# VectorE forms the delta-net output's low parts, layer 1 walks its keys by token tile, and the result leaves through transposes of the updated x

## The chip, the cores and the metric

The kernel runs on one core of one Trainium2 chip. The metric is the device time of one execution in microseconds (us); smaller is better. TensorE (PE) does the matmuls, VectorE (DVE), ScalarE (ACT) and GpSimd (POOL) the elementwise work, and SyncE (SP) issues the DMAs. A change of under about 0.2% (4 us) can't be told from no change in this kernel's measurements.

## The reference

Two layers (shared by a context pass of 128 tokens and a denoising step of 256 latent tokens, so 384 tokens in all, of width 1024). Per layer, cut to what matters:

```
mod = silu(cond) @ w_mod + b_mod                    # shift, scale, gate of both halves
h = rmsnorm(x) * (1 + sc1) + sh1
(dq, dk, dv, ..., aq, ak, av, mg) = split(h @ w_in)  # 13 parts
o_dn = rmsnorm(gated_delta_rule(...)) * silu(dgate)  # 8 heads of 128
y_a = o_dn @ w_br_dn                                 # delta net
y_b = (sb * conv3(scg * sx)) @ w_br_sc               # gated short convolution
y_c = attention(rope(norm(aq)), rope(norm(ak)), av) @ w_br_att
mix = (g_a*y_a + g_b*y_b + g_c*y_c) @ w_out
x = x + gt1 * rmsnorm(mix)
x = x + gt2 * rmsnorm(relu(h2 @ w_up)**2 @ w_down)   # h2: x normed and modulated again
```

The outputs are x after layer 1 (for both passes) and the context's keys, values and delta-net states.

## The kernel before, in words

**Tiles.** The 384 tokens are 3 token tiles of 128 (t = 0 context, t = 1, 2 latent). `xm` (tile name XT in the trace) holds x with tokens on partitions, 128 x 1024 for each token tile. `om` (tile name OT there) holds the output of a sub-layer in the same layout, and the name OT also serves `ot[f]`, the delta net's output of head f with channels on partitions, 128 x 384. PSUM tiles are `mm` (accumulators of the large products) and `ax` (small ones).

**Precision.** Each large product of fp32 operands is three fp32r matmuls: high x high, high x low, low x high. A high part is a cast (`ah`, `HH`, `wh`), a low part is the difference of the value and its high part (`al`, `HL`, `wl`). Weights come by DMA into `wr` (4 buffers); ACT casts `wh` and DVE subtracts `wl` (3 buffers each). `split(k, src)` does the same for an activation: ACT casts `ah`, POOL subtracts `al`. Small products are plain fp32 matmuls. One fp32 matmul is two MATMUL instructions in the trace, and one transpose is one instruction; the listing of an engine's instruction order, further down, counts each of either once.

**The modulation** of a layer is worked out while the layer before it (or the first half of the same layer) runs. Pieces of `w_mod` come through the same `wr` buffers. DVE sums them into `macc` (TENSOR_SCALAR and SCALAR_TENSOR_TENSOR, 128 x 1024), and 16 narrow matmuls `ax<-macc,one` add up the partitions; other pieces go to PE as they are, 16 at a time (8 in some places), as `ax<-wr,csil`. In the code both are the matmuls with a `tile_position`.

**Order.** All operations are recorded first, each with a class (`rec.cls`). `schedule()` then lists them engine by engine, with the durations that `cost()` gives and with the priority offsets of `PAR["off"]`; the resulting order of each engine is fixed, and only semaphores decide when an instruction starts. So a cost or a class that is changed moves instructions elsewhere too. `warmup()` gives one matmul on `ones` that the scheduler repeats in places where PE would idle at the end of the program; `cold(...)` names the last operation that they may precede.

**The keys of the attention** (`TM("k", l, 0, 272, evac_k)`): three weight pieces of `w_in` (816, 816 and 544 columns, so 3, 3 and 2 of the 8 blocks of 128 rows) times the three token tiles; 272 columns are 256 of keys and 16 of gates. The walk goes piece by piece: piece 0 for tiles 0, 1, 2, then piece 1, then piece 2, and with piece 2 each tile's sums are complete and `evac_k` norms and rotates the keys (`junk`, `kss`, `kn`, `ku`). The values follow in the same way (`evac_v`).

**The end.** After the last product of layer 1's MLP (`mm<-wh,u` and `mm<-wl,u`, 512 columns), each token tile goes through a chain: DVE multiplies the sums into `om`, ACT sums squares, DVE adds (m), POOL raises to the power -1/2, DVE refines by one Newton step (y, z in `ns`), and `finish_y` forms x + om * (z*y) and turns it, so that it is written with channels on partitions: 8 fp32 matmuls `xm` x ident start the sums (`ax<-ident,XT`), and 8 with the diagonal of z*y (`dg`) add om (`ax<-dg,OT`). ACT and DVE copy the two banks to `yst`, and a DMA writes them. A line of the profile's L1778 is the recorder's; every operation has it, so the tiles' names tell them apart.

Of the kernel before, what the change touches and what calls it, by code (L numbers as in the profile page):

```python
# [9 lines left out]
F32 = mybir.dt.float32  # L10
# [4 lines left out]
ADD, SUB, MUL = ALU.add, ALU.subtract, ALU.mult  # L15

P = 128
# [162 lines left out]
def cost(op, method, outs, ins, tag):  # L180

    n = max(size(v) for v in outs[:1] + ins)
    ps = any(tag.get(v.tensor.name) in PSUM_TAGS for v in outs + ins)
    if op.eng == "PE":
        n = size(outs[0])
        if tiled(op, ins):
            if "tile_position" in op.k:
                return n * 4 / 2.4 + 3 if op.k["tile_position"] == (0, 0) else 27.0
            return 43.0 if n <= 32 else 71.0
        if method == "transpose":  # L190
            return n * 2 / 2.4 + 3
        if ins[0].dtype == F32R and n >= 256:
            return n / 2.4 + 13.8
        return max(214.0, n * 4 / 2.4 + 3)
    if op.eng == "ACT":
        c = 51 + n * 0.833 + (0 if ps else 42)
        c += 93 * sum(isap(op.k.get(x)) for x in ("bias", "scale")) + 93 * (method == "mul")
        return c + (93 if "accum_out" in op.k else 0)
    if op.eng == "DVE":
        if method == "reciprocal":  # L200
            return 69 + 6.25 * n
        fast = method in ("tensor_scalar", "tensor_copy") and not ps
        sc = sum(isap(op.k.get(x)) for x in ("scalar", "scalar1", "scalar2"))
        return 69 + n * 1.042 * (0.5 if fast else 1) + 58 * sc
    if op.eng == "POOL":
        if method == "memset":
            return 35 + n * 0.833
        if method == "affine_select":
            return 160 + n * 0.83
        if method == "tensor_copy":  # L210
            return 250 if n <= 96 else 345
        return (165 + n * 2.1) if op.k.get("op") != ALU.pow else 300 + 165 * n
    return max(56.0, n * outs[0].shape[0] * 4 / 360.0)
# [24 lines left out]
def schedule(rec, par):  # L238
# [54 lines left out]
    while done < len(ops):  # L293
# [114 lines left out]
        **{(e, "w"): o for e, o in (("ACT", -500), ("DVE", 550), ("SP", 300))},  # L408
        **{(e, "bg"): o for e, o in (("PE", 950), ("DVE", 400), ("POOL", 800))},
        **{(e, "hv"): 1500 for e in ("PE", "ACT", "DVE")},  # L410
        ("DVE", "mv"): -200, ("DVE", "me"): 1000, ("PE", "gemm"): -1500,
    },
    "margin": 300.0, "gmargin": 0.0,
# [7 lines left out]
def build(tc, aps):  # L421
    nc = tc.nc
    rec = Recorder()
    PE, ACT, DVE, POOL, SP = (Eng(rec, n, r) for n, r in (
        ("PE", nc.tensor), ("ACT", nc.scalar), ("DVE", nc.vector), ("POOL", nc.gpsimd), ("SP", nc.sync)))
# [19 lines left out]
    def axtile():  # L445
        return pax.tile([P, 512], F32, tag="ax", name="ax")
# [41 lines left out]
    S = {}  # L488
# [89 lines left out]
                      start=True, stop=True)  # L578
        return rb

    def split(k, src):
        ACT.copy(a_hi[k], src)
        POOL.tensor_tensor(out=a_lo[k], in0=src, in1=a_hi[k].bitcast(F32), op=SUB)

    def warmup():

# [8 lines left out]
    def cold(first):  # L595
        if "fill" in S:
            S.pop("fill").last = rec.ops[first]
# [17 lines left out]
    def X(fn, *a):  # L615
        items.append(((), lambda _: fn(*a)))
# [26 lines left out]
    def G(keys, fn):  # L643
        items.append((tuple(keys), fn))
# [9 lines left out]
            rec.cls = "bg"  # L654
        G([("w", l, row)], run)

    def TM(kind, l, g, n, evac):

        st = {}

        parts = KPARTS if kind == "k" else HALVES

        def part(j):
            def run(ch):
                hi, lo = ch[0]
                if j == 0:
                    st["ps"] = [bank(), mmtile(), mmtile()]
                first = len(rec.ops)
                for t in range(3):
                    ps = st["ps"][t]  # L670
                    rec.cls = "gemm"
                    for i, k in enumerate(parts[j]):
                        ah = h_hi[k][:, t * P:(t + 1) * P]
                        al = h_lo[k][:, t * P:(t + 1) * P]
                        wh, wl = hi[:, i * n:(i + 1) * n], lo[:, i * n:(i + 1) * n]
                        PE.matmul(ps[:, :n], lhsT=ah, rhs=wh, start=k == 0, stop=False)
                        PE.matmul(ps[:, :n], lhsT=ah, rhs=wl, start=False, stop=False)
                        PE.matmul(ps[:, :n], lhsT=al, rhs=wh, start=False, stop=k == 7)
                    cold(first)
                    rec.cls = "bg"  # L680
                    if k == 7:
                        rec.cls = "ev"
                        evac(t, ps)
                        rec.cls = "bg"
            return run
        for j in range(len(parts)):
            G([(kind, l, g, j)], part(j))

    def TMW(keys, acts, evac, tail=False, after=None):

# [283 lines left out]
    def newton(n, c):  # L974

        rec.cls = "step" + S["u"]
        a, b, y, z, m = (n[:, c + j:c + j + 1] for j in range(5))
        DVE.tensor_tensor(out=m, in0=a, in1=b, op=ADD)
        POOL.tensor_tensor(out=y, in0=m, in1=mhalf, op=ALU.pow)
        DVE.scalar_tensor_tensor(out=z, in0=y, scalar=-0.5, in1=y, op0=MUL, op1=MUL)  # L980
        DVE.tensor_scalar(out=z, in0=z, scalar1=m, scalar2=1.5, op0=MUL, op1=ADD)
        return y, z

    def diag(t, y, z):
        dg = S["dg"][:, t]
        DVE.tensor_scalar(out=dg, in0=ident, scalar1=z, scalar2=y, op0=MUL, op1=MUL)
        rec.cls = "crit" + S["u"]
        return dg

    def finish_y(t, n):  # L990

        banks = [axtile() for _ in range(2)]
        cols = [(slice(f * P, (f + 1) * P), banks[f // 4][:, f % 4 * P:f % 4 * P + P]) for f in range(8)]
        for f, c in cols:
            PE.matmul(c, lhsT=xm[:, t, f], rhs=ident, start=f.start % 512 == 0, stop=False)
        dg = diag(t, *newton(n, 0))
        for f, c in cols:
            PE.matmul(c, lhsT=om[:, t, f], rhs=dg, start=False, stop=f.stop % 512 == 0)
            if t == 2 and f.start == 512:
                cold(len(rec.ops) - 1)  # L1000
        for g, ps in enumerate(banks):
            y4 = S["yst"][:, 4 * g:4 * g + 4, t * P:(t + 1) * P]
            p4 = ps.rearrange("p (f c) -> p f c", f=4)
            if g:
                DVE.tensor_copy(y4, p4)
            else:
                ACT.copy(y4, p4)
            SP.dma_start(aps["y"][:, 4 * g:4 * g + 4, t * P:(t + 1) * P], y4)
# [49 lines left out]
    def layer(l):  # L1058
# [518 lines left out]
        def evac_y(f, first):  # L1577
# [6 lines left out]
                    POOL.tensor_tensor(out=mix, in0=mix, in1=th, op=ADD)  # L1584
            return run

        def split_mix(f):
            DVE.tensor_scalar(out=xt[f], in0=xt[f], scalar1=0.5, scalar2=None, op0=MUL)
            split(f, xt[f])
# [27 lines left out]

        if l == 0:
            qkv(0)
        TM("k", l, 0, 272, evac_k)  # L1620
        TM("k", l, 1, 272, evac_v)
        X(gates)

# [43 lines left out]
                JOIN(("da", l, h))  # L1667
        spread = modlist(l, "M") if l == 0 else []
        for f in range(8):
            X(lambda f=f: split(f, ot[f]))  # L1670
        m2 = list(spread)

        due = [0.0]
# [200 lines left out]
```

## Time and profile before

| | |
|---|---|
| median of 3 runs | 1985.2 us (1985.07 to 1986.72) |
| the profiled execution | 1986.29 us, of which the span of the trace 1984.6 us |
| granted TensorE clock, mean | 0.997 |
| PE busy | 1957.0 us (99%) |
| DVE, ACT, POOL busy | 1405.9, 949.3, 431.6 us |
| moved by DMA | 280 MB, 141 GB/s on average |

Durations in a row are those of the instruction alone; PE pipelines its matmuls, so the time that one costs PE is the distance to the start of the next. In a timeline row "x8" groups 8 instructions that follow each other; the bracket at its end is the idle time of the engine before it, and what ended that.

### The profile page before, as it was taken

To read this page: it belongs to the slowest core of one execution; us is meant where nothing else is said; L and a number is where in the kernel's file an instruction comes from. 1 tells how busy PE (TensorE), PEld (TensorE's weight loads), DVE (VectorE), ACT (ScalarE), POOL (GpSimd) and SP (SyncE) were. 2 spreads that over 40 slices of the span, in tenths; PEclk is the share of its full clock that TensorE was granted. 3 is DMA by queue.
4 is the path that set the end of the run, shared out by engine and by line. 5 is a ranking of instruction groups with operands and counts; after the bars stand their busy time and mean duration, and the time that the engine had idled before them with its cause. 6 is when DMAs were issued, how large, how long until landed. Compare 5 with 4: busy or idle time off the path is not lost.

```text
span 1984.6 us, 35881 instructions
## 1 busy us (share of the span) xinstructions
PE 1957.0 (99%) x12980; PEld 1806.7 (91%) x12980; DVE 1405.9 (71%) x4317; ACT 949.3 (48%) x2188; POOL 431.6 (22%) x666
## 2 busy tenths in 40 slices
PE   9999999999999999999999999999999999999999
PEld 6998999999998799779779989999999998898987
DVE  3798887988868589769557988779888545432433
ACT  4676644555542354334246665445555424443432
POOL 1222222123234313003012022222232322110210
PEclk9999999999999999999999999999999999999999
DMA  8522333333336837756654223333333334554352
GB/s 270 192 81 84 106 110 130 119 122 117 107 124 208 289 128 231 217 189 204 158 177 147 85 94 115 111 119 122 121 115 107 120 123 144 195 124 128 127 128 64
DMA packets 132385, 280.48 MB, mean 141 GB/s; under 512 B 12240, under 2 KB 80496, under 8 KB 132208
## 3 DMA queue, kind: packets, MB, share of 16 engines
q1 hardware_dynamic: 132208, 278.19, 43.0%
q8 instruction: 102, 1.67, 0.3%
q14 instruction: 75, 0.61, 0.1%
HBM read 270.73 MB, written 7.42 MB: 140 GB/s over the span
## 4 chain that ended last, share of the span: by engine, by line
PE 83%; DVE 7%; DMA 4%; ACT 3%; issue 2%; POOL 0%; SPq 0%; DVEq 0%; ACTq 0%
PE mm L1778 70%; PE ax L1778 14%; DMA wr<-in_wmod 3%; DVE wl L1778 2%; DVE macc L1778 2%; ACT E L1778 1%; DVE q L1778 1%; ACT wh L1778 0%; DVE MB L1778 0%; ACT ht L1778 0%; ACT junk L1778 0%; DVE Xc L1778 0%; DVE Pr L1778 0%; DVE XT L1778 0%; DMA ws<-in_wmod 0%
## 5 line engine op out<-in xcount | busy, mean ns | idle before, releaser
L1778 DVE TENSOR_TENSOR wl<-wr,wh 128x1024 fp32r<-128x1024 f32 (+2 forms) x380 | 478.7, 1261 | 307.0 <-ACT wh L1778 305.8
L1778 ACT CAST wh<-wr 128x1024 fp32r<-128x1024 f32 (+2 forms) x380 | 396.0, 1043 | 559.3 <-PE mm L1778 454.1
L1778 PE MATMUL mm<-HH,wl 128*128 128x384 f32 x1664 | 568.9, 342 | 1.7 <-DVE wl L1778 1.7
L1778 PE MATMUL mm<-HL,wh 128*128 128x384 f32 x1664 | 567.7, 341 | 0.0
L1778 PE MATMUL mm<-HH,wh 128*128 128x384 f32 x1664 | 564.9, 340 | 0.6 <-ACT HH L1778 0.6
L1778 PEld LDWEIGHTS mm<-HH,wl 128*128 128x128 f32 x1664 | 312.9, 188 | 9.6 <-issue 4.5
L1778 PEld LDWEIGHTS mm<-HL,wh 128*128 128x128 f32 x1664 | 312.8, 188 | 6.5 <-issue 3.9
L1778 PEld LDWEIGHTS mm<-HH,wh 128*128 128x128 f32 x1664 | 312.4, 188 | 5.7 <-issue 1.2
L1778 DVE SCALAR_TENSOR_TENSOR macc<-wr,csil,macc 128x1024 f32<-128x1024 f32 x98 | 144.9, 1512 | 26.7 <-DMA wr<-in_wmod 26.7
L1778 PE MATMUL mm<-wh,HH 128*128 128x256 f32 (+1 forms) x480 | 139.9, 292 | 2.1 <-DVE eq L1778 1.4
L1778 PE MATMUL mm<-wl,HH 128*128 128x256 f32 (+1 forms) x480 | 139.4, 291 | 1.3 <-DVE wl L1778 1.3
L1778 PE MATMUL mm<-wh,HL 128*128 128x256 f32 (+1 forms) x480 | 140.1, 292 | 0.0
L1778 DVE TENSOR_TENSOR Pr<-MB,Xc 128x6 f32<-128x6 f32 (+30 forms) x496 | 138.7, 280 | 0.3
L1778 DVE TENSOR_REDUCE Xc<-Pr 128x6 f32<-128x12 f32 (+30 forms) x496 | 127.4, 257 | 7.7
L1778 DVE STREAM_SHUFFLE MB<-Mc 128x6 f32<-128x6 f32 (+30 forms) x496 | 131.7, 272 | 0.0
L1778 PE MATMUL mm<-al,wh 128*128 128x384 f32 x384 | 129.9, 339 | 1.6 <-POOL al L1778 1.5
L1778 PE MATMUL mm<-ah,wl 128*128 128x384 f32 x384 | 130.0, 339 | 0.2 <-DVE wl L1778 0.2
L1778 PE MATMUL mm<-ah,wh 128*128 128x384 f32 x384 | 130.0, 339 | 0.0
L1778 PE MATMUL mm<-wh,u 128*128 128x512 f32 x384 | 124.0, 399 | 0.0
L1778 PE MATMUL mm<-wh,ah 128*128 128x512 f32 x288 | 112.9, 392 | 0.0
L1778 PE MATMUL mm<-wh,al 128*128 128x512 f32 x288 | 112.7, 391 | 0.0
L1778 PE MATMUL mm<-wl,ah 128*128 128x512 f32 x288 | 112.5, 390 | 0.0
(270 smaller groups left out, 3314.8 us busy)
## 6 DMA issues: line engine op xcount, KB each, us to landing
wr<-in_wf SPq DMA_DIRECT2D x336, 512.0 KB, 3.3
wr<-in_wmod SPq DMA_DIRECT2D x80, 512.0 KB, 4.2
wr<-in_wq SPq DMA_DIRECT2D x16, 512.0 KB, 3.4
wr<-in_wdg SPq DMA_DIRECT2D x16, 512.0 KB, 3.3
ws<-in_wmod SPq DMA_DIRECT2D x16, 384.0 KB, 7.0
E<-scr SPq DMA_DIRECT2D x16, 384.0 KB, 3.6
Qe<-scr SPq DMA_DIRECT2D x16, 256.0 KB, 3.8
wr<-in_wkv SPq DMA_DIRECT2D x8, 408.0 KB, 5.7
```

What stands on the lines that cost most here:

```text
L1778: o.call(*o.a, **o.k)
```

## The change

Four edits.

1. `cost()`: a narrow matmul at `tile_position` (0, 0) is taken for 0.965 ns a column instead of 1.667. No instruction is added or removed by it; the scheduler's order changes.
2. The low parts of the delta net's output (8 for each layer, `al<-OT,ah`, 128 x 384) are subtracted by DVE instead of POOL, under a class "sp" of its own with an offset of 1000 on ACT and DVE.
3. In layer 1 the key product is walked by token tile: all 24 matmuls of tile 0 over the three weight pieces, then tile 1, then tile 2.
4. `finish_y`: DVE forms r = z*y and adds om * r into xm in two halves (SCALAR_TENSOR_TENSOR, 128 x 512), and 8 PE transposes turn the new xm; the 16 fp32 matmuls and the diagonal are gone.

```diff
@@ cost
-                return n * 4 / 2.4 + 3 if op.k["tile_position"] == (0, 0) else 27.0
+                return n * 0.965 + 3 if op.k["tile_position"] == (0, 0) else 27.0
@@ PAR["off"]
+        **{(e, "sp"): 1000 for e in ("ACT", "DVE")},
@@
-    def split(k, src):
+    def split(k, src, eng=POOL):
         ACT.copy(a_hi[k], src)
-        POOL.tensor_tensor(out=a_lo[k], in0=src, in1=a_hi[k].bitcast(F32), op=SUB)
+        eng.tensor_tensor(out=a_lo[k], in0=src, in1=a_hi[k].bitcast(F32), op=SUB)
@@ TM
-                hi, lo = ch[0]
...
-                    for i, k in enumerate(parts[j]):
...
+                    for (hi, lo), j in zip(ch, js):
+                        for i, k in enumerate(parts[j]):
...
-        for j in range(len(parts)):
-            G([(kind, l, g, j)], part(j))
+        n_ = len(parts)
+        for js in [tuple(range(n_))] if whole else [(j,) for j in range(n_)]:
+            G([(kind, l, g, j) for j in js], part(js))
@@ finish_y
-        banks = [axtile() for _ in range(2)]
-        cols = [(slice(f * P, (f + 1) * P), banks[f // 4][:, f % 4 * P:f % 4 * P + P]) for f in range(8)]
-        for f, c in cols:
-            PE.matmul(c, lhsT=xm[:, t, f], rhs=ident, start=f.start % 512 == 0, stop=False)
-        dg = diag(t, *newton(n, 0))
-        for f, c in cols:
-            PE.matmul(c, lhsT=om[:, t, f], rhs=dg, start=False, stop=f.stop % 512 == 0)
...
+        y, z = newton(n, 0)
+        r = n[:, 5:6]
+        DVE.tensor_tensor(out=r, in0=z, in1=y, op=MUL)
+        rec.cls = "crit" + S["u"]
+        for g in range(2):
+            ps = axtile()
+            h = slice(512 * g, 512 * g + 512)
+            DVE.scalar_tensor_tensor(out=xm[:, t, h], in0=om[:, t, h], scalar=r, in1=xm[:, t, h], op0=MUL, op1=ADD)
+            for j in range(4):
+                f = 4 * g + j
+                PE.transpose(ps[:, j * P:(j + 1) * P], xm[:, t, f * P:(f + 1) * P], ident)
...
@@ layer
+        def split_out(f):
+            rec.cls = "sp"
+            split(f, ot[f], DVE)
+            rec.cls = "bg"
...
-        TM("k", l, 0, 272, evac_k)
+        TM("k", l, 0, 272, evac_k, l > 0)
...
-            X(lambda f=f: split(f, ot[f]))
+            X(lambda f=f: split_out(f))
```

What the order of instructions becomes is shown at three places. First the end of PE's list, before; `mm<-wh,u` and `mm<-wl,u` are the last products of the MLP, `ax<-dg,OT` and `ax<-ident,XT` those of finish_y, `mm<-ones` the fillers:

```order
L1778 MATMUL ax<-dg,OT 128x128 x8
L1778 MATMUL ax<-ident,XT 128x128 x4
L1778 MATMUL ax<-dg,OT 128x128
L1778 MATMUL ax<-ident,XT 128x128 x4
L1778 MATMUL ax<-dg,OT 128x128 x7
L1778 MATMUL mm<-wl,u_3838 128x512
L1778 MATMUL mm<-wh,u_3838 128x512
L1778 MATMUL mm<-wh,u_3839 128x512
L1778 MATMUL mm<-wl,u_3839 128x512
L1778 MATMUL mm<-wh,u_3839 128x512
L1778 MATMUL mm<-ones 128x128 x17
L1778 MATMUL ax<-dg,OT 128x128 x8
```

The same end of PE's list, after:

```order
L1789 MATMUL mm<-wl,u_3838 128x512
L1789 MATMUL mm<-wh,u_3838 128x512
L1789 MATMUL mm<-wh,u_3839 128x512
L1789 MATMUL ax<-ident,XT 128x128 x4
L1789 MATMUL mm<-wl,u_3839 128x512
L1789 MATMUL ax<-ident,XT 128x128 x4
L1789 MATMUL mm<-wh,u_3839 128x512
L1789 MATMUL mm<-ones 128x128 x12
L1789 MATMUL ax<-ident,XT 128x128 x4
L1789 MATMUL mm<-ones 128x128 x5
L1789 MATMUL ax<-ident,XT 128x128 x4
L1789 MATMUL mm<-ones 128x128 x3
```

(A last `ax<-ident,XT` x8 follows.) Before, 24 fp32 matmuls stand ahead of the last five products; after, 8 transposes stand among them, and those of tile 1 stand among the fillers. The four groups of 4 `ax<-ident,XT` matmuls of tiles 0 and 1, which stood some 250 us ahead of the end in PE's list, have gone.

Second, DVE at the end of layer 0's delta net, before (`wl` and `macc` are the weights' low parts and the modulation's sums, `mgth` a gate):

```order
L1778 TENSOR_TENSOR wl<-wr,wh 128x1024
L1778 SCALAR_TENSOR_TENSOR mgth<-mgth,mm 128x384
L1778 SCALAR_TENSOR_TENSOR macc<-wr,csil,macc 128x1024 x4
L1778 TENSOR_TENSOR wl<-wr,wh 128x1024 x2
L1778 SCALAR_TENSOR_TENSOR macc<-wr,csil,macc 128x1024 x4
```

And after:

```order
L1789 TENSOR_TENSOR wl<-wr,wh 128x1024
L1789 TENSOR_TENSOR al_123<-OT,ah_115 128x384
L1789 TENSOR_TENSOR al_124<-OT,ah_116 128x384
L1789 TENSOR_TENSOR al_125<-OT,ah_117 128x384
L1789 TENSOR_TENSOR al_126<-OT,ah_118 128x384
L1789 TENSOR_TENSOR al_127<-OT,ah_119 128x384
L1789 TENSOR_TENSOR al_128<-OT,ah_120 128x384
L1789 TENSOR_TENSOR al_129<-OT,ah_121 128x384
L1789 SCALAR_TENSOR_TENSOR macc<-wr,csil,macc 128x1024
L1789 TENSOR_TENSOR al_130<-OT,ah_122 128x384
L1789 SCALAR_TENSOR_TENSOR macc<-wr,csil,macc 128x1024 x3
L1789 SCALAR_TENSOR_TENSOR mgth<-mgth,mm 128x384
```

The eight subtractions now stand ahead of the four sums and of the two `wl` that follow them.

Third, ACT at the start of layer 1's keys, before (`junk,kss` sums squares of the keys of one tile, `bt` its gates):

```order
L1778 COPY modrow<-ax 128x256
L1778 CAST wh<-wr 128x816
L1778 ACTIVATE junk,kss<-mm 128x128 x2
L1778 ACTIVATE bt<-mm 128x16
L1778 ACTIVATE junk,kss<-mm 128x128 x2
L1778 ACTIVATE bt<-mm 128x16
L1778 CAST wh<-wr 128x816
L1778 ACTIVATE bt<-mm 128x16
L1778 CAST wh<-wr 128x544
```

And after:

```order
L1789 ACTIVATE junk,kss<-mm 128x128 x2
L1789 ACTIVATE bt<-mm 128x16
L1789 ACTIVATE junk,kss<-mm 128x128 x2
L1789 ACTIVATE bt<-mm 128x16
L1789 ACTIVATE KTA<-ax,gqc 128x2x128
L1789 COPY modrow<-ax 128x256
L1789 CAST wh<-wr 128x816
L1789 ACTIVATE bt<-mm 128x16
L1789 ACTIVATE junk,kss<-mm 128x128
L1789 CAST wh<-wr 128x816
L1789 ACTIVATE junk,kss<-mm 128x128
L1789 CAST wh<-wr 128x544
```

The evacuations of tiles 0 and 1 now come ahead of the copy of `modrow`, and the three casts of the values' weights come behind it, one by one between those of tile 2.

## Rows read from the trace of the kernel before

**Rows 1.** The page: PE's busy time, and the chain that ended last by engine.

```profile
PE   1957.0 (99%) x12980; PEld 1806.7 (91%) x12980; DVE 1405.9 (71%) x4317; ACT 949.3 (48%) x2188; POOL 431.6 (22%) x666
...
PE 83%; DVE 7%; DMA 4%; ACT 3%; issue 2%; POOL 0%; SPq 0%; DVEq 0%; ACTq 0%
```

**Rows 2.** PE's waits by what ended them: us in total, times, longest.

```profile
PE ax L1778 <- DVE macc L1778: 7.9, 4, 4.2
...
PE mm L1778 <- POOL al L1778: 1.5, 2, 1.1
```

**Rows 3.** PE timeline, 33 us, then 1695 to 1708: start, us, instruction, [idle].

```profile
33.09 1.47 PE L1778 MATMUL ax<-ident,XT 128*128 128x128 f32 x12
...
1695.12 1.05 PE L1778 MATMUL ax<-ident,XT 128*128 128x128 f32 x8
...
1698.48 0.64 PE L1778 MATMUL ax<-wr,csil 128*32 128x256 f32 x8 [1.01 <-DMA wr<-in_wmod]
...
1706.66 1.05 PE L1778 MATMUL ax<-ident,XT 128*128 128x128 f32 x8
1707.55 0.38 PE L1778 MATMUL ax<-ident,modrow 128*128 128x128 f32 x2
```

**Rows 4.** PE timeline, the end of the program.

```profile
1968.13 1.95 PE L1778 MATMUL ax<-dg,OT 128*128 128x128 f32 x16
1969.91 1.10 PE L1778 MATMUL ax<-ident,XT 128*128 128x128 f32 x8
...
1973.45 0.48 PE L1778 MATMUL mm<-wl,u 128*128 128x512 f32 x1
...
1974.70 3.96 PE L1778 MATMUL mm<-ones 128*128 128x128 f32 x34
1978.49 1.99 PE L1778 MATMUL ax<-dg,OT 128*128 128x128 f32 x16
```

**Rows 5.** DVE timeline, the end of the program; then one group: busy, mean ns | idle.

```profile
1970.11 0.69 DVE L1778 COPY yst<-ax 128x512 f32<-128x512 f32 x1
...
1974.90 0.69 DVE L1778 TENSOR_TENSOR OT<-mm,OT 128x512 f32<-128x512 f32 x1 [0.48 <-PE mm L1778]
...
1977.58 0.16 DVE L1778 SCALAR_TENSOR_TENSOR ns<-ns 128x1 f32<-128x1 f32 x1 [0.44 <-POOL ns L1778]
...
1980.52 0.69 DVE L1778 COPY yst<-ax 128x512 f32<-128x512 f32 x1 [2.14 <-PE ax L1778]
...
L1778 DVE SCALAR_TENSOR_TENSOR XT<-OT,ns,XT 128x512 f32<-128x512 f32 x18 | 12.9, 748 | 0.3
```

**Rows 6.** Timelines of POOL, DVE and PE, 596 to 625; last a group of DVE.

```profile
598.38 9.78 POOL L1778 TENSOR_TENSOR al<-OT,ah 128x384 fp32r<-128x384 f32 x5
...
596.17 7.26 DVE L1778 SCALAR_TENSOR_TENSOR macc<-wr,csil,macc 128x1024 f32<-128x1024 f32 x4
...
620.30 4.87 DVE L1778 SCALAR_TENSOR_TENSOR macc<-wr,csil,macc 128x1024 f32<-128x1024 f32 x4 [0.94 <-DMA wr<-in_wmod]
...
604.33 0.44 PE L1778 MATMUL mm<-al,wh 128*128 128x384 f32 x1 [1.11 <-POOL al L1778]
...
605.41 0.45 PE L1778 MATMUL mm<-HH,wl 128*128 128x384 f32 x1 [0.29 <-DVE wl L1778]
...
608.22 0.45 PE L1778 MATMUL mm<-al,wh 128*128 128x384 f32 x1 [0.43 <-POOL al L1778]
...
L1778 DVE TENSOR_TENSOR al<-ax,ah 128x384 fp32r<-128x384 f32 x16 | 8.8, 552 | 5.4 <-ACT ah L1778 5.4
```

**Rows 7.** PE timeline, layer 1's keys, 1019 to 1050.

```profile
1028.69 0.64 PE L1778 MATMUL ax<-wr,csil 128*32 128x256 f32 x8 [0.95 <-DMA wr<-in_wmod]
...
1041.35 0.39 PE L1778 MATMUL mm<-wl,HH 128*128 128x272 f32 x1 [1.26 <-DVE wl L1778]
```

**Rows 8.** PE timeline; then a stretch: us, PE, PEld, DVE, ACT, POOL busy, PE clock, DMA.

```profile
853.30 1.06 PE L1778 MATMUL ax<-macc,one 128*32 128x256 f32 x2 [4.18 <-DVE macc L1778]
...
853.00:860.00 7.00, 6.70 (x26) 3.42 (x27) 2.58 (x3) 0.37 (x1) 0.00 (x0) 0.53 0.47 162
```

More of the change, by code (lines that the diff above doesn't have):

```diff
@@ L655, in FM, with TM, part @@
         G([("w", l, row)], run)
-    def TM(kind, l, g, n, evac):
+    def TM(kind, l, g, n, evac, whole=False):
         st = {}
         parts = KPARTS if kind == "k" else HALVES
-        def part(j):
+        def part(js):
             def run(ch):
-                hi, lo = ch[0]
-                if j == 0:
+                if js[0] == 0:
                     st["ps"] = [bank(), mmtile(), mmtile()]
@@ L671, in run @@
                     rec.cls = "gemm"
-                    for i, k in enumerate(parts[j]):
[L673 to L678, printed above, removed]
+                    for (hi, lo), j in zip(ch, js):
+                        for i, k in enumerate(parts[j]):
+                            ah = h_hi[k][:, t * P:(t + 1) * P]
+                            al = h_lo[k][:, t * P:(t + 1) * P]
+                            wh, wl = hi[:, i * n:(i + 1) * n], lo[:, i * n:(i + 1) * n]
+                            PE.matmul(ps[:, :n], lhsT=ah, rhs=wh, start=k == 0, stop=False)
+                            PE.matmul(ps[:, :n], lhsT=ah, rhs=wl, start=False, stop=False)
+                            PE.matmul(ps[:, :n], lhsT=al, rhs=wh, start=False, stop=k == 7)
                     cold(first)
@@ L990, in finish_y @@
     def finish_y(t, n):
-        banks = [axtile() for _ in range(2)]
-        cols = [(slice(f * P, (f + 1) * P), banks[f // 4][:, f % 4 * P:f % 4 * P + P]) for f in range(8)]
-        for f, c in cols:
-            PE.matmul(c, lhsT=xm[:, t, f], rhs=ident, start=f.start % 512 == 0, stop=False)
-        dg = diag(t, *newton(n, 0))
-        for f, c in cols:
-            PE.matmul(c, lhsT=om[:, t, f], rhs=dg, start=False, stop=f.stop % 512 == 0)
-            if t == 2 and f.start == 512:
-                cold(len(rec.ops) - 1)
-        for g, ps in enumerate(banks):
+        y, z = newton(n, 0)
[9 more added lines that the diff above has]
+                PE.transpose(ps[:, j * P:(j + 1) * P], xm[:, t, f * P:(f + 1) * P], ident)
+                if t == 2 and f == 4:
+                    cold(len(rec.ops) - 1)
             y4 = S["yst"][:, 4 * g:4 * g + 4, t * P:(t + 1) * P]
```

## The prediction

> **What bounds the kernel now.** I read the page first: PE is busy for 99% of the span, and the chain that ended last runs 83% through PE and 7% through DVE [rows 1]. Three readings follow. An instruction taken out of PE's list saves its distance to the next one's start, unless PE then waits for what follows. What DVE, ACT or POOL do is free, unless PE waits for it. And a shorter wait saves what it shortens. So I next read PE's waits: `macc` on DVE costs most, 7.9 us in 4 waits with the longest at 4.2; POOL's `al`, which edit 2 touches, costs 1.5 in 2 [rows 2]. Last I read the timelines of the stretches that the change touches, each engine beside the others: PE some 280 us before the end [rows 3], the end [rows 4, 5], layer 0's delta-net output [rows 6], layer 1's keys [rows 7].
>
> The sum is made against the profiled execution, 1986.29 us, of which the span is 1984.6 and 1.7 lies around it. It is 1.1 above the median of the runs, 1985.2, so 1.1 comes off at the end. About 0.2%, 4 us, is what a measurement can tell from no change.
>
> **Edit 4, away from the end.** The `ident` matmuls of tiles 0 and 1 are started early, in the middle of the MLP's products: 4 groups of 4 matmuls (x8 in the trace, two instructions each). One group starts at 1706.66, the next instruction at 1707.55: 0.89 us of PE [rows 3]. PE is the bound there, with matmuls on either side, so 4 x 0.89 = 3.6 us go. Behind the first of these groups stands a `ax<-wr,csil` that waits 1.01 us for its DMA at 1698.48 [rows 3]. PE would reach it 0.89 earlier and wait longer, were it not that edit 1 moves it behind some 6 to 9 more products. I estimate that 0.4 of that wait goes (0 to 1.0). Together -4.0.
>
> **Edit 4, at the end.** Before, PE spends 1968.13 to 1973.45, 5.3 us, on 24 fp32 matmuls (tile 0's and 1's with `dg`, tile 2's with `ident`) ahead of the last five products, which take 1973.45 to 1974.70 [rows 4]. Only those products complete tile 2's sums. After, 8 transposes stand among them. The nearest row for a transpose is the turning of x at the start, 12 in 1.47 us, 0.12 each or less [rows 3]: 8 cost at most 1.0. So the products are through at 1968.13 + 1.25 + 1.0 = 1970.4, 4.3 us earlier than 1974.70.
>
> What is late next is DVE, whose list I replay. It now does r and two halves x + om*r for each tile; such a half is in the trace in the other sub-layers, 748 ns [rows 5]. Tile 0's second half ends at about 1969.1, its transposes at 1970.1, and its copy to `yst` (0.69, as at 1970.11 [rows 5]) stands ahead of tile 2's first step, which so starts at 1970.85, against 1974.90 [rows 5]. Before, from there to the Newton step took 1977.58 - 1974.90 = 2.7 us [rows 5]; one of tile 1's halves now stands inside and adds up to 0.75 less what waits there anyway: Newton at 1973.9. Then 0.4 for it and r, two halves at 0.75, so tile 2's new x is ready at 1975.7.
>
> PE meanwhile has 20 fillers at 3.96/17 = 0.23 us [rows 4], 4.7 us, and 8 transposes of tile 1 at 0.12, 1.0: from 1970.4 it is free at 1976.0. The two paths end almost together. Then 8 transposes, to 1976.9, and the last copy starts near 1977.0 instead of 1980.52 [rows 5]: **-3.6**. The copy and the DMA behind it are the same. If the halves cost more or the replay slips by one instruction of 0.75, -2.8; if fillers are no obstacle, -4.2. The cover of the early transposes is thin: each 0.1 that PE or DVE loses here is lost at the end.
>
> **Edit 2.** In layer 0, POOL makes 8 low parts, the last 5 in 9.78 us, 1.96 each, while DVE's sums beside them take 7.26/4 = 1.82 each; where POOL is idle, at 620, they take 4.87/4 = 1.22 [rows 6]. PE waits for the last low parts and for a `wl` that DVE is late with: 1.11 + 0.29 + 0.43 = 1.8 us [rows 6]. After, DVE does them: the nearest DVE row is the same subtraction from PSUM, 552 ns [rows 6], so 8 cost 4.4 us. Queued behind them are four sums and two `wl`. But the sums get back 4 x 0.6 = 2.4 when POOL stands aside, and seven low parts fit into idle time that DVE has before the sums start. By that the low parts are there by 598, the sums end near 601.5 instead of 603.4, and `wl` behind them is ready before its use at 605.4. The three waits vanish: **-1.8**. Bounds: -2.3 (the small gaps around them go too), and, if the sums' chain is later by all of the 4.4 less 2.4, +2.0 wherever PE next waits for `macc`. At 620.30 DVE waits 0.94 for a DMA [rows 6], so a part of such a delay would be absorbed; I stay near the gain. In layer 1 PE shows no wait of this kind (both in rows 2's count are in layer 0), so edit 2 is worth nothing there.
>
> A rule speaks against this edit. The Trainium skill, "Perfetto Trace Analysis", section "Optimizing Scalar/DVE Operations", says that DVE and GpSimd share an SBUF read port, so that moving operations between those two might not help. By it edit 2 would be worth 0 instead of -1.8, and the result 1.8 later. The rows agree with the sharing (1.82 against 1.22), and just for that reason I expect a gain here: the same subtraction takes 1.96 on POOL and 0.55 on DVE, so moving it ends the sharing sooner.
>
> **Edit 3.** In layer 1, tile 0's keys are complete some 10 us earlier, since PE doesn't walk all three tiles first. The number of matmuls is the same. Before, PE waits 0.95 for a `ax<-wr,csil` and 1.26 for the values' first `wl` [rows 7]; the latter because ACT casts the values' weights only after it has copied `modrow`, and DVE subtracts after that. After, the casts stand behind the same copy and behind tile 0's and 1's evacuations, and the keys' `wh` buffers come free only in tile 2's walk. So the wait of 1.26 shrinks, as DVE has less else to do then, but it doesn't go. I estimate 0.6 of it left, and 0.3 of the wait of 0.95 gone with the later place: **-0.9**, between +0.6 (ACT's casts late by another 1.5) and -2.2 (both waits gone). POOL and DVE now rotate tile 0's keys earlier, and the delta net's first heads of layer 1 are reordered behind that; that is worth 0 on PE as long as PE has products to do, and I leave 1 us either way.
>
> **Edit 1.** No work changes. Some groups of narrow matmuls stand a few products later in PE's list, which helps where they wait for a DMA or for `macc` [rows 2] and hurts nothing that PE waits for. But DVE's orders change too (two `wl` in a row where one was). A product of 384 columns is 0.17 us, so a group that moves by three gains 0.5 where it waits, and there are the 4 for `macc` [rows 2] and a few like that of 0.95 [rows 7], of which one is long: at 853.30 PE waits 4.18 us for `macc`, and its clock then is at 0.53 for the 7 us from 853, the lower of its two levels for most of it (1.2 of 2.4 GHz), which costs another 7 x 0.47 = 3.3 [rows 8]. That wait comes from DVE waiting for a DMA, and moving the group by a few products shortens it by as much. I take **-0.5**, from -2 to +2 without that wait.
>
> The sum: 4.0 + 3.6 + 1.8 + 0.9 + 0.5 = 10.8. 1986.3 - 10.8 = 1975.5, less 1.1 is 1974.4; I say **1974.5 us**.
>
> **The rivals.**
> (A) The forecast, 1974.5, chance 0.54.
> (B) Only edit 4 counts; what edits 2, 3 and 1 gain is given back where PE next waits for `macc`, because its chain (DMA, sums, next DMA into the buffer that a sum has freed) is serial and doesn't hang on PE. For it: the largest wait is of that chain [rows 2]. Against it: DVE's sums get faster by edit 2. 1986.3 - 7.6 - 1.1 = 1977.6, chance 0.25.
> (C) The clock. In the last stretch transposes take the place of fp32 matmuls. If PE's clock fell on them, as it did behind the 4.18 us of waiting [rows 8], 24 transposes of 0.12 would take twice as long: up to 2.9 on the end, 1 at least for the last 8, which nothing covers. 1975.5 to 1977.4, chance 0.07. The Trainium skill, "TensorE: Matmul & The Clock Gate", section "Part 4: PE-mode transpose", says that a transpose doesn't count as PE being busy in the way a matmul does. Against it: the 12 transposes at 33 us show no more than 0.12 each [rows 3], and at the end fillers stand between.
> (D) The long wait goes. If the sums reach PE in time at 853, 4.2 + 3.3 = 7.5 go as well [rows 8]: 1967.0, chance 0.05. For it: edit 2 takes POOL off DVE's back. Against it: that is 250 us earlier.
> (E) The slower end: DVE's 4.4 us in layer 0 stand ahead of the sums, the buffers that these free are refilled later, and further groups `ax<-macc,one` wait as the one at 853 does, each with the wait and the clock behind it, 7.5 us [rows 8]. One such wait gives 1982.0, within 0.2%; two give 1989.5, slower. From a delay of the chain of 4 us or more it decides; my replay gives less than 0. Chances 0.05 and 0.03.
> (F) The change doesn't do what it says at the end: the transposes wait for DVE's halves ahead of the products that follow them in PE's list, so the last products are late by as much, and the end gains only 1 us instead of 3.6: 1977.1, chance 0.01 beyond what B holds.
>
> **How the numbers follow.** Range: the low end takes edits 1 to 3 at their good bounds (2.3, 2.2 and 2, so 3.3 more than in the sum) and the end at -4.2: near 1970.5, and I go to 1970.0. The high end takes B and the bad bounds of edits 2 and 4 (2.0 and 0.8): 1980.4, so 1980.5. D and E, 0.13, lie outside. Faster by over 0.2% (under 1981.2): A, B, C, D and F, 0.92, of which I move 0.03 to the same for noise in the sum: 0.89. Within 0.2%: one wait of E and that, 0.08. Slower: 0.03.
>
> **What the profile after would show.** Right: no `ident` groups near 1700, and PE's list shorter by 3.6 there; the last copy about 3.5 earlier relative to the last products of tile 1; no wait for `al` near 604 and sums of 1.2 us there; a wait of about half a us or less at the values' first `wl`; the wait at 850 still about 4. Wrong: further waits `PE ax <- DVE macc`; a clock below 0.9 in the last 10 us ahead of the last transpose; transposes of tile 0 that wait for XT; a new wait in layer 1's delta-net heads. The forecast is wrong above all if the order that edit 1 gives meets the DMAs differently at 853: one such wait more or less is as much as two thirds of the sum.

## The result, and the profile after

The changed kernel takes 1964.6 us (median of 4 runs, 1964.1 to 1966.2), against 1986.0 for the kernel before (4 runs); the ratio is 0.990, with an interval from 0.988 to 0.992. That is 21 us by the medians (20 by the ratio) where the prediction had 11, and below the range, whose low end was 1970.0. The profiled execution has a span of 1962.4 us against 1984.6, which is 22.2 less. A second series, on another occasion, gave 0.989 (0.987 to 0.991).

The page, PE's busy time and the chain that ended last by engine, of the changed kernel (as [rows 1]):

```profile
PE 1944.9 (99%) x12922; PEld 1797.9 (92%) x12922; DVE 1415.9 (72%) x4339; ACT 948.4 (48%) x2188; POOL 404.9 (21%) x650
...
PE 85%; DVE 7%; DMA 3%; ACT 3%; issue 1%; POOL 1%; SPq 0%; DVEq 0%; ACTq 0%; POOLq 0%
```

PE is the bound as before, busy for 12 us less and idle for 10 less. Its waits (as [rows 2]):

```profile
PE ax L1789 <- DVE macc L1789: 3.8, 4, 2.1
...
PE mm L1789 <- DVE wl L1789: 1.0, 2, 0.6
```

`macc` has gone from 7.9 to 3.8, and `al` is no longer in the list.

To see where the 22 us lie I took, from both traces, the start of the same large product (the n-th `mm` matmul, fillers not counted; there are 9024 in each) at some places, and compared how long the stretches between them last. All tables below are made so, in us against the profiled execution of before; the stretches are named by its times.

| stretch | what is there | change |
|---|---|---|
| 0 to 588 | start, layer 0's heads (edit 1 changes orders up to 50) | -2.3 |
| 588 to 656 | delta net's output split (edit 2) | -4.0 |
| 656 to 818 | layer 0's merge, MLP | +0.4 |
| 818 to 873 | layer 0's MLP: the long wait for `macc` | -6.1 |
| 873 to 1007 | layer 0's MLP | -0.7 |
| 1007 to 1320 | layer 1's keys, first heads (edits 3, 1) | -2.7 |
| 1320 to 1663 | layer 1 | +0.7 |
| 1663 to 1724 | early groups of finish_y, some 280 us ahead of the end (edit 4) | -4.6 |
| 1952 to the end | the end (edit 4) | -3.0 |

**The end.** PE's timeline there (as [rows 4]), and DVE's (as [rows 5]):

```profile
1949.62 0.60 PE L1789 MATMUL ax<-ident,XT 128*128 128x128 f32 x4
1949.97 0.48 PE L1789 MATMUL mm<-wl,u 128*128 128x512 f32 x1
...
1950.96 2.84 PE L1789 MATMUL mm<-ones 128*128 128x128 f32 x24
1953.64 0.60 PE L1789 MATMUL ax<-ident,XT 128*128 128x128 f32 x4
...
1955.62 0.83 PE L1789 MATMUL mm<-ones 128*128 128x128 f32 x6
1956.30 1.08 PE L1789 MATMUL ax<-ident,XT 128*128 128x128 f32 x8
```

```profile
1951.53 0.68 DVE L1789 TENSOR_TENSOR OT<-mm,OT 128x512 f32<-128x512 f32 x1
...
1955.19 1.42 DVE L1789 SCALAR_TENSOR_TENSOR XT<-OT,ns,XT 128x512 f32<-128x512 f32 x2
1956.52 0.68 DVE L1789 COPY yst<-ax 128x512 f32<-128x512 f32 x1
1957.42 0.69 DVE L1789 COPY yst<-ax 128x512 f32<-128x512 f32 x1 [0.21 <-PE ax L1789]
```

Four transposes take 1949.97 - 1949.62 = 0.35 us of PE, 0.09 each. With 19.2 us off by then, tile 2's first step at 1951.53 stands where 1970.7 would be before (1970.85 in the prediction), the last halves end at 1956.6 or 1975.8 (1975.7), the last copy starts at 1957.42 or 1976.6 (1977.0). The replay held to within 0.4 us. The span gains 0.9 less than the copy does: 4.3 us lie between the end of the last copy and the end of the span, before 3.4. In the trace of before the two last copies end 5.8 us or more behind those of tile 1; now the last three end within 1 us, and their DMAs of 256 KB follow each other. That the last DMA takes longer for this reason is argued, not tested.

**Where edit 2 is.** DVE and POOL in the stretch of [rows 6]:

```profile
591.27 3.36 DVE L1789 TENSOR_TENSOR al<-OT,ah 128x384 fp32r<-128x384 f32 x7
...
596.22 3.67 DVE L1789 SCALAR_TENSOR_TENSOR macc<-wr,csil,macc 128x1024 f32<-128x1024 f32 x3
```

The subtractions take 3.36/7 = 0.48 each, the sums 3.67/3 = 1.22, as where POOL was idle before, and PE doesn't wait there at all (590 to 620).

**The long wait.** The counterparts of [rows 8], PE's timeline and the same stretch of the program:

```profile
844.23 0.62 PE L1789 MATMUL ax<-macc,one 128*32 128x256 f32 x2 [0.99 <-DVE macc L1789]
...
853.00:860.00 7.00, 7.00 (x33) 5.82 (x33) 3.71 (x3) 3.14 (x5) 0.00 (x0) 1.00 0.45 157
```

0.99 us instead of 4.18, and a clock of 1.00 behind it instead of 0.53. The prediction held it for unlikely (D, 0.05) and had priced it at 7.5 us. It is one execution; further on, a second trace of the same kernel has the wait again.

### The profile page after: what moved, and what is told of

Its sections match the earlier page's. It is cut to its first block, busy times and chain, and to the rows that moved or that the text cites. A ratio compares the mean times of both kernels' runs of the same rounds, so it can differ in the third digit from the quotient of the medians.

```text
span 1962.4 us, 35757 instructions
## 1 busy us (share of the span) xinstructions
PE 1944.9 (99%) x12922; PEld 1797.9 (92%) x12922; DVE 1415.9 (72%) x4339; ACT 948.4 (48%) x2188; POOL 404.9 (21%) x650
## 4 chain that ended last, share of the span: by engine, by line
PE 85%; DVE 7%; DMA 3%; ACT 3%; issue 1%; POOL 1%; SPq 0%; DVEq 0%; ACTq 0%; POOLq 0%
PE mm L1789 72%; PE ax L1789 14%; DVE wl L1789 2%; DMA wr<-in_wmod 2%; DMA wr<-in_wf 1%; DVE macc L1789 1%; ACT wh L1789 1%; DVE MB L1789 1%; DVE Xc L1789 1%; DVE Pr L1789 1%; POOL xe L1789 0%; ACT E L1789 0%; ACT ht L1789 0%; DMA E<-scr 0%; DVE XT L1789 0%
```

## The experiments

Ratios are to the kernel before, run beside each kernel on the same chip, with their 95% intervals; 1% is 20 us. The kernel before had medians of 1987 to 1989 us there, between 1980 and 1998.

### Each edit alone

Only the lines of one edit of the diff are in each of these four.

**Edit 1** (`n * 0.965 + 3` in `cost()`):

> Edit 1 alone: only the cost of the narrow matmuls in the planner is changed, so the order of PE, DVE, SP and ACT differs, mostly in layer 0's MLP and from layer 1's keys on. Theory 1 (the 4.18 us wait for macc near 850 and the half clock behind it went because edit 1 puts wl and macc in another order on DVE there): the wait at 850 falls to about 1 us with the clock at 1.0, and the time is 6 to 8 us below before. Theory 2 (it went because edit 2 relieves DVE at 600 and the chain of sums arrives earlier): the wait stays near 4 us and the time is within 2 us of before. Theory 3 (the wait comes and goes from run to run, whatever the kernel): the two traces disagree with the timed runs.

Measured: 0.9955 (0.9942 to 0.9967), some 9 us. Other than the description of the change says, the edit does add instructions: the planner sets four more fillers (`mm<-ones`, 294 instructions in the trace instead of 286), in the first 26 us.

**Edit 2** (`split_out`):

> Edit 2 alone: the low parts of the delta net's output on DVE, all else as before. Both theories: no wait for al near 604, 3 to 4 us gained by 620. Theory 1: the wait near 850 stays about 4 us with the half clock behind it, time 2 to 4 us below before. Theory 2: the wait near 850 falls to about 1 us, time 8 to 10 us below before.

Measured: 0.9985 (0.9976 to 0.9994), some 3 us.

**Edit 3** (`TM(..., l > 0)`):

> Edit 3 alone: layer 1's keys walked by token tile. My sum had 0.9 us for it (from +0.6 to -2.2). The trace of the whole change shows about 1.9 less between 1010 and 1095, part of which may be edit 1's: expected 0.5 to 2 us below before. Theory 1 and theory 2 alike: the wait near 850 stays at about 4 us, since nothing ahead of 1010 is different.

Measured: 0.9978 (0.9965 to 0.9990), some 4 us.

**Edit 4** (`finish_y`):

> Edit 4 alone: the end through VectorE and transposes. My sum had 3.6 for the early groups and 3.6 at the end, 0.4 for a DMA wait: 7.2 to 7.6 us below before. If the DMA wait behind the first of the early groups grows by what the group took (0.9) as nothing shifts the group of narrow matmuls, 6.3 to 6.7. The wait near 850 stays at about 4 us.

Measured: 0.9969 (0.9957 to 0.9981), some 6 us.

The four ratios multiply to 0.989, which is what the whole change has: within the intervals (0.001 for each edit, 0.002 for the whole) the edits add up, and no gain is seen that only their combination brings. The largest is edit 1, for which the sum had 0.5 us. By stretches:

| stretch | edit 1 | edit 2 | edit 3 | edit 4 | whole |
|---|---|---|---|---|---|
| 588 to 656 | +0.6 | -4.1 | -0.2 | +0.7 | -4.0 |
| 656 to 818 | -0.3 | +1.2 | +1.4 | +2.8 | +0.4 |
| 818 to 873 | -5.6 | -2.2 | -4.6 | -3.8 | -6.1 |
| 1007 to 1320 | -2.0 | -0.1 | -3.1 | +0.2 | -2.7 |
| 1320 to 1663 | +0.9 | +0.1 | +0.7 | +0.1 | +0.7 |
| 1663 to 1724 | -1.0 | +0.3 | +1.1 | -4.2 | -4.6 |
| 1952 to the end | 0.0 | 0.0 | 0.0 | -3.0 | -3.0 |

Edits 2 and 4 have their places, to 0.5 us. But edits 3 and 4 change no order ahead of 1007, and yet gain 4 us at 818 to 873. So the profiled execution of before was a bad one there, and one trace of each kernel isn't enough to read that stretch. This is what the next runs are for.

### The same kernels again, and edit 1 in halves

A second trace of the kernel before:

> The kernel before once more, for a second trace. Its orders are those of before, so any difference of stages is what one execution differs from another. Theory 1 (the long wait near 850 belongs to the order of before): the wait for macc there is again 2.5 us or more, with or without the half clock. Theory 3 (it comes by chance whatever the order): it may be 1 to 1.6, as in the two traces that have edit 1.

The whole change without edit 1:

> The whole change without edit 1 (costs of the narrow matmuls as before). If the edits add up by their own runs (0.9955 x 0.9985 x 0.9978 x 0.9969 = 0.989 for all), this one has a ratio near 0.993, 13 to 14 us below before, and its wait for macc near 840 is 2.5 us or more. If edit 2 or 4 removes the wait too, the time is within 2 us of the whole change (ratio 0.99) and the wait is near 1.

Measured: 0.9927 (0.9910 to 0.9944), as the edits' own ratios gave. PE's wait that ends at 849.5 is 3.0 us. So edits 2 to 4 don't bring edit 1's gain.

Edit 1 for the matmuls on `macc` alone, and for those on the weight pieces alone:

```diff
-                return n * 4 / 2.4 + 3 if op.k["tile_position"] == (0, 0) else 27.0
+                c = 0.965 if any("macc" in v.tensor.name for v in ins) else 4 / 2.4
+                return n * c + 3 if op.k["tile_position"] == (0, 0) else 27.0
```

> Edit 1 for the matmuls on macc alone: the other narrow matmuls keep the cost of before. It changes the orders in layer 0's MLP (some 50 rows of PE, 40 of DVE) and little else. Theory 1: the wait near 850 falls to 1 to 1.6 us with the clock at 1.0, 3 to 6 us gained between 818 and 873, nothing elsewhere. If not the order there but the other narrow matmuls bring edit 1's gain: within 1 us of before outside of that stretch and no gain in it.

Measured: 0.9967 (0.9952 to 0.9982), some 6.5 us; the other half, with `not any(...)`:

> Edit 1 for the narrow matmuls on the weight pieces alone (those on macc keep the cost of before). It changes the orders from layer 1's keys on. Theory 1: the wait near 850 stays at 2.5 us or more; 0.5 to 1.5 us gained at the keys and 1 us near 1697, at most 2 to 3 us below before.

Measured: 0.9976 (0.9963 to 0.9990), some 5 us, more than expected; its trace shows only 2.4, of which 1.7 at 1007 to 1663.

Edit 1, the whole change and before once more, and the whole change without edit 3:

> Edit 1 alone once more, beside these on the same chip, for a second ratio and a second trace. Expected: ratio 0.994 to 0.997; waits for macc near 806 and 850 of 3 to 5.5 us in all, against 4.5 to 6 in the traces of the old order. If its trace shows half a clock behind 850 like two of the five traces that have edit 1, the gain is in how often that happens and not in each execution.

> The whole change once more, for a second trace and on the same chip as the others. Theory 1: the wait for macc near 843 is below 1.7 us and the clock from 838 to 868 is 1.0 again; ratio 0.988 to 0.992. Theory 3: the wait may be 2.6 us or more with half a clock.

> The kernel before, a third trace. Expected: the wait for macc near 850 at 2.6 us or more, with half a clock in two cases of three.

> The whole change without edit 3 (layer 1's keys walked by weight piece). If edits 1 and 3 both reorder the same stretch and don't add up (each alone gains 1.7 to 2.0 us between 1007 and 1663, both together 1.9), then this one is within 1 us of the whole change in its trace from 1007 on, and its ratio is 0.989 to 0.992. If edit 3 is worth the 4 us that its own run shows, it is 3 us or more behind the whole change.

Measured: edit 1 again 0.9970 (0.9957 to 0.9982); the whole change again 0.9892 (0.9871 to 0.9914); without edit 3 0.9903 (0.9880 to 0.9926), 3 us behind the whole change by medians of the same occasion (1968.7 and 1965.8), with intervals that overlap.

The long wait, in the traces with the old order in layer 0's MLP: 4.18 (before), 2.83 and 2.94 (before again), 3.63 (edit 1 for pieces), 3.3 (edit 2), 2.48 (edit 3), 3.26 (edit 4), 3.0 (without edit 1). Of before again, PE's row, and the stretch 840 to 870:

```profile
850.30 1.06 PE L1778 MATMUL ax<-macc,one 128*32 128x256 f32 x2 [2.83 <-DVE macc L1778]
...
840.00:870.00 30.00, 27.16 (x119) 20.13 (x118) 16.72 (x19) 7.56 (x10) 0.00 (x0) 0.89 0.61 193
```

With the new order: 0.99 (whole), 1.45 and 1.18 (edit 1, twice), 1.38 (edit 1 for `macc`), but 2.90 (whole again) and 2.42 (without edit 3). Of edit 1 for `macc`, and of the whole change again:

```profile
848.80 0.62 PE L1779 MATMUL ax<-macc,one 128*32 128x256 f32 x2 [1.38 <-DVE macc L1779]
...
840.00:870.00 30.00, 28.62 (x143) 23.17 (x142) 19.93 (x22) 8.95 (x12) 0.00 (x0) 1.00 0.67 209
```

```profile
850.29 0.75 PE L1789 MATMUL ax<-macc,one 128*32 128x256 f32 x2 [2.90 <-DVE macc L1789]
...
840.00:870.00 30.00, 27.11 (x126) 20.81 (x125) 17.36 (x20) 7.49 (x10) 0.00 (x0) 0.94 0.62 193
```

So the new order doesn't remove the wait; it is shorter in most traces (a mean of 1.7 in six against 3.2 in the eight of the old order), and the clock falls less often behind it (in 2 of the six, in 6 of the eight). Both traces with a long wait and a fall have edit 1 together with others; in the three with edit 1 or its half for `macc` alone the wait is 1.2 to 1.5, and the clock stays.

Taking the mean of three traces of before and of two of edit 1, edit 1 gains 7.9 us: 4.4 at 818 to 873, 1.4 at 1663 to 1724, 1.7 at 1007 to 1320 less 0.8 that comes back behind, and 1.2 at 60 to 100; the other stretches cancel. The 1.2 are mostly a wait of PE for DVE's `eq` near 65 us; in the first trace of before, then of edit 1:

```profile
PE mm L1778 <- DVE eq L1778: 1.4, 1, 1.4
```

```profile
PE mm L1778 <- DVE eq L1778: 0.2, 1, 0.2
```

That wait is 0.2 in seven of the eight traces that have the new cost for the weight pieces (0.7 in the eighth), and 0.5 to 1.4 in the ten others.

How the order does it is to be seen on DVE. Before (second trace), layer 0's MLP:

```profile
820.32 1.28 DVE L1778 SCALAR_TENSOR_TENSOR macc<-wr,csil,macc 128x1024 f32<-128x1024 f32 x1 [2.23 <-DMA wr<-in_wmod]
821.52 1.22 DVE L1778 TENSOR_TENSOR wl<-wr,wh 128x1024 fp32r<-128x1024 f32 x1
822.65 1.27 DVE L1778 SCALAR_TENSOR_TENSOR macc<-wr,csil,macc 128x1024 f32<-128x1024 f32 x1
```

The same place with edit 1 for `macc`:

```profile
819.58 1.23 DVE L1779 TENSOR_TENSOR wl<-wr,wh 128x1024 fp32r<-128x1024 f32 x1 [2.67 <-ACT wh L1779]
820.72 2.47 DVE L1779 SCALAR_TENSOR_TENSOR macc<-wr,csil,macc 128x1024 f32<-128x1024 f32 x2
```

Before, DVE stands 2.23 us at a sum whose weight piece is still on its way, with a `wl` behind it that could be done in the last 0.7 us (ACT's cast for it, 818.54 and 1.05 long, ends at 819.59), and the two sums of one piece lie on both sides of that `wl`. In the other order `wl` is done while the piece lands, and the two sums follow without a wait. What counts is the buffer that this `wl` frees, as SP's and DVE's rows show: the DMA of a later piece of `w_mod` starts right behind its end. Of before again, then of edit 1 for `macc`:

```profile
822.76 0.34 SPq L1778 DMA_DIRECT2D wr<-in_wmod  x1
...
848.97 2.48 DVE L1778 SCALAR_TENSOR_TENSOR macc<-wr,csil,macc 128x1024 f32<-128x1024 f32 x2 [1.67 <-DMA wr<-in_wmod]
```

```profile
820.83 0.34 SPq L1779 DMA_DIRECT2D wr<-in_wmod  x1
...
847.46 2.48 DVE L1779 SCALAR_TENSOR_TENSOR macc<-wr,csil,macc 128x1024 f32<-128x1024 f32 x2 [1.88 <-DMA wr<-in_wmod]
```

The two executions are level there (the cast at 818.54 and at 818.50), and that DMA starts 1.9 us earlier. So the chain is serial: piece, its first sum, the `wl` behind that, a later piece. At its end the last two sums start 1.5 us earlier, and PE's wait is shorter by as much (1.38 for 2.83).

### The order of sums and `wl` set by hand

This applies to before only what was seen on DVE: PE's, ACT's and SP's orders stay.

```diff
+    for a, b, c in zip(dve, dve[1:], dve[2:]):
+        if b.outs[0].startswith("wl") and sums(a) and sums(a) == sums(c):
+            order.remove(a)
+            order.insert(order.index(b) + 1, a)
```

> The kernel before with only DVE's order altered by hand at three places of layer 0's MLP: where one of the two sums of a weight piece stands ahead of a wl and the other behind it, the first is moved behind that wl, so DVE no longer waits for the piece's DMA with a ready wl behind it, and the piece's buffer is free about 0.6 us earlier each time. PE's, ACT's and SP's orders are those of before. Theory 1 (edit 1 gains near 850 by DVE's order of sums and wl): the wait for macc near 850 falls from 2.6 to 4.3 us to 1 to 2 us, the clock from 840 to 870 stays at 1.0, 3 to 5 us below before. Rival (what counts is PE's place of the narrow matmuls, or SP's order): the wait stays at 2.6 us or more, within 1 us of before.

The long wait is gone in this trace, by DVE's order alone, where the eight traces of the old order have 2.48 to 4.18; PE's row, and the stretch:

```profile
852.42 0.62 PE L1790 MATMUL ax<-macc,one 128*32 128x256 f32 x2
...
840.00:870.00 30.00, 29.86 (x143) 23.59 (x142) 19.88 (x22) 9.35 (x11) 0.00 (x0) 1.00 0.67 211
```

The stretch 818 to 873 gains 6.9 against the profiled execution of before, 5.5 against the mean of its three traces. But the ratio is 0.9984 (0.9969 to 0.9999), some 3 us: in the trace 656 to 818 loses 5.0, where the wait ahead of the long one has the clock's fall behind it:

```profile
809.83 1.03 PE L1790 MATMUL ax<-macc,one 128*32 128x256 f32 x2 [2.17 <-DVE macc L1790]
...
795.00:820.00 25.00, 22.83 (x103) 17.11 (x102) 19.11 (x19) 6.54 (x8) 1.64 (x1) 0.93 0.69 201
```

DVE's order up to 800 is that of before, so 2.7 of the loss, which lie ahead of 728, aren't this move's; whether the other 2.3 are, one trace doesn't tell. The wait of 2.17 is within what the old order has at this place (1.25 to 2.44). The fall of the clock behind it is seen in five traces of kernels with another order (this one, the next one, the whole change again, without edit 3, and half the sums with the old costs) and in none of the eight. The same move on the whole change:

> The whole change with the same move on DVE at the four places where its order still splits a pair of sums. Theory 1: the wait near 845 (1.15 us) and the one at 803 (2.08) fall by 0.3 to 1 together, no clock to win back: 0 to 1 us below the whole change, so a ratio near 0.99 to before. Rival: no difference.

Measured: 0.9900 (0.9877 to 0.9922), 1968.2 us where the whole change beside it has 1965.8: no gain. Its wait near 848 is 0.22, and at 656 to 818 it is 2.0 above the first trace of the whole change, but 1.1 below the second, which hasn't this move. So it isn't shown that the chain gives back at one place what it wins at the other.

### The chain made slack

If edit 1 gained by that chain alone, its gain would vanish where the chain is short in both orders. Here 42 of the 98 sums are left out, in before and in edit 1:

```diff
+                if seen[o.outs[0]] < 7 and o.k["scalar"].offset % 2:
+                    continue
```

> The kernel before with 42 of the 98 sums that DVE adds up for the modulation left out (the second column of each piece but the first and the last), every other instruction in the order of before. Its output is therefore not the reference's. Each weight piece's buffer is read once instead of twice and is free 1.2 us earlier. Theory 1 (the chain piece, sums, next piece sets PE's waits for macc at 660, 806, 850 and 952): these waits fall from 8.6 us in all to below 2, the clock stays at 1.0 behind them, and the time is 8 to 12 us below before. Rival (the DMA alone sets them): the waits stay above 5 us in all.

> Edit 1 alone with the same 42 sums left out, so its output is not the reference's either. Theory 1 (edit 1 gains by shorter waits in that chain): with the chain slack in both, edit 1 is worth only what it changes elsewhere, at the keys and near 1697: 1 to 3 us less than the kernel with half the sums and the old costs. Rival (edit 1's 6 to 9 us lie elsewhere): it is 5 us or more below that kernel.

Measured: 0.9956 (0.9942 to 0.9970) and 0.9932 (0.9916 to 0.9948), medians of 1977.5 and 1972.1. Half the sums are worth 9 us of before. In the trace 6.6 us are gained at the long wait, so the chain is a bound there, and 2.6 at 588 to 656, where POOL and DVE work beside each other. Edit 1 keeps 5 us on top of that, at the border of what the rival expected. PE's waits, with the old costs and with edit 1:

```profile
PE ax L1784 <- DMA wr<-in_wmod: 2.7, 6, 1.0
PE ax L1784 <- DVE macc L1784: 2.7, 2, 2.4
```

```profile
PE ax L1784 <- DVE macc L1784: 2.2, 2, 1.7
...
PE ax L1784 <- DMA wr<-in_wmod: 1.3, 2, 0.8
```

The long wait is 0.40 and 0.55 us. What edit 1 still gains is in the groups that wait for a DMA of a weight piece (6 waits, 2.7 us in all, become 2 with 1.3), in layer 1's keys (2.2 us at 1007 to 1320), and 2.2 us at 728 to 818, where the old order has a wait of 2.4 with a lower clock behind it. That last wait is for `macc` too, so the chain wasn't slack in the first of the two kernels, and they don't separate it from the rest; the keys and the groups are gains beside it.

## Why the prediction was right and wrong

**What bounds the kernel:** right. PE is busy for 99%, and each gain is PE's list or PE's waits.

**Edit 4:** right in its two terms and in size: 7.6 in the sum, 7.1 in the trace of edit 4 alone, 7.6 in that of the whole change. The early groups and the DMA wait behind them gave 4.2 to 4.6 for 4.0, the end 3.0 for 3.6. That the total agrees to the tenth is luck: the errors of the two terms cancel, and in the whole change the 4.6 hold some of what edit 1 alone gains there (1.0). What the replay lacked is the last step: it took the DMA behind the last copy as unchanged, and it takes 0.9 longer, now behind two others. The copy itself came 0.4 earlier than replayed.

**Edit 2:** the mechanism was right (the sums are back at 1.22, the waits gone), the size too small: 4.0 at its place for 1.8. I took the three named waits and left the rest as a bound of 2.3; the gaps around them and the wait of 0.72 for `wl` at 616 went as well. Over the whole program it measures 3 us (1 to 5). That it would cost the chain of sums was a bound of mine that did not come about: DVE's sums there end at 599.9 in the trace after, or 602.2 with the 2.3 us that the program is ahead by then, against 603.4 before.

Moving work from POOL to DVE helped by 4 us at its place: the same subtraction takes 0.48 on DVE and took 1.96 on POOL, beside sums of 1.82 instead of 1.22. The rule that spoke against edit 2, the Trainium skill, "Perfetto Trace Analysis", section "Optimizing Scalar/DVE Operations", says that such a move might not help. For this edit it doesn't hold.

**Edit 3:** 0.9 in the sum; its own trace has 2.3 (3.1 less 0.7 that comes back), its ratio 4 us (2 to 7). The wait of 1.26 at the values' `wl`, of which I left 0.6, is not in the waits of edit 3's own trace, so that one guess was short there; in the whole change 0.40 of it is left. In the heads behind (1050 to 1320), which I put at 0 within 1, 1.8 us were gained in its own trace, less the 0.7. On top of edit 1 it is worth 1.1 to 1.8 in the traces and 3 by the medians, which can't be told from the 4.

**Edit 1:** the step that failed. It measures 6 to 9 us where the sum has 0.5. I saw the long wait, its price, and that it comes from DVE waiting for a DMA, and then looked at how far the narrow matmuls move in PE's list (three products, 0.5 us). What mattered is what the planner does elsewhere when a cost is changed: on DVE, `wl` and sums stand in another order, and the wait is at the end of a serial chain of pieces, which runs 1.5 us ahead in the trace above. I had named that ("DVE's orders change too") and priced it at nothing. In the traces this place has 4.4 of edit 1's 7.9; the other 3.5 are in three places at or behind groups on the weight pieces that moved (60 to 100, the keys, 1663 to 1724), where I had a bound of 2. That DVE's order shortens the wait is shown by the order set by hand; that this gives all of the 4.4 in time is not, since that kernel gained 3 us (0.2 to 6).

**The rivals.** D happened in the profiled execution, for another reason than the one I gave: the kernels without edit 1 still wait 2.5 to 4.2 us, so edit 2 didn't do it. It doesn't happen in every execution: the second trace of the whole change has a wait of 2.90, and with 1970.4 us it is the slowest of its five. B, that the chain gives the gains back, isn't borne out: 656 to 818 is 1 to 5 us longer in ten of the other traces, but two of them are those of edits 3 and 4, whose orders there are before's (1.4 and 2.8), and the times of the edits add up. C did not happen: with 20 transposes in it, the stretch 1950 to 1957 has a clock of 1.00:

```profile
1950.00:1957.00 7.00, 7.00 (x62) 6.82 (x61) 6.59 (x17) 1.96 (x5) 1.36 (x2) 1.00 0.38 115
```

The rule behind C, the Trainium skill, "TensorE: Matmul & The Clock Gate", section "Part 4: PE-mode transpose", can't be told right or wrong by it, since matmuls and fillers stand between the transposes. E and F are not in the times.

**The reference trace.** The sum was made against one execution. In the stretch 818 to 873 that execution was the slowest of all the traces of the old order, by 0.6 to 4.6 us. For the terms of edits 2 to 4 this made no difference; for the long wait it decides what "before" is.

**What stays open.** How edit 1's 6 to 9 us of time divide between the chain and the groups that wait for a piece's DMA: the means of few traces give 4.4 and 3.5, single executions of one kernel differ by up to 3.4 at 818 to 873, and the runs with half the sums leave it 5 us without the long wait. Why the clock falls behind some of the waits: it fell behind 2.42, 2.83, 2.90 and 4.18 us near 850 and behind 1.89 to 2.87 near 807, and did not behind 3.26 (edit 4) and 2.48 (edit 3), so the length of the wait alone doesn't decide it.

## What to carry to other kernels

Where a planner sets the order, a changed cost is an edit of every engine's order: compare the orders of the engine that the largest waits name, not only those of the engine whose cost was changed. In an in-order queue, work that is ready should stand ahead of work that waits for a transfer, above all where it frees a buffer that the next transfer needs: here that took away the long wait in both kernels in which it was done by hand, though only one of them gained time, 3 us. And a wait at the end of such a chain is to be read in several traces: here it was 0.99 and 2.90 us in two executions of one kernel, and its stretch differed by 3.4 us.

## What the runs showed of the hardware

A wait of 2 to 4 us on PE in the middle of its work was in some executions followed by several us at a lower granted clock (0.89 to 0.94 on average over 25 or 30 us where it fell, 1.00 where it didn't). By these shares the fall costs 1.8 to 3.3 us, about as much as the wait. A transpose of 128 x 128 in fp32 took 0.09 us of PE's list, against 0.22 for the fp32 matmul that did the same. And in the traces of edit 1 and of the order set by hand, whose orders at 602 are those of before, PE waits 2.2 us for `wl` there, where the three traces of before wait 1.1 for `al` instead: of POOL and DVE, which share the stretch, either one was the later.
